# A mixer block's inverse and buffers on one core: second buffers for five tiles, other PSUM banks for late products, and the triangular inverse with its backward half mirrored

## The chip, the core and the metric

One core of a Trainium2 chip runs the whole program. The metric is the device time of one execution in microseconds (us); the time before the change is 2026.64 us, the median of 3 runs (2023.53 to 2029.68).

## What is computed

One layer of a flow-matching backbone over 256 latent tokens and 256 context tokens of width 2048, all in float32. The context tokens are mixed first; each latent scan starts from the context's final state.

```python
o_c, ctx_states = _mix(_modnorm(h_c, norm1_g, m_c[0], m_c[1]), CTX_LEN, zero, lp)
o_x, _ = _mix(_modnorm(h_x, norm1_g, m_x[0], m_x[1]), GRID_W, ctx_states, lp)
h_x = h_x + m_x[2] * o_x
h_x = h_x + m_x[5] * _swiglu(_modnorm(h_x, norm2_g, m_x[3], m_x[4]), ffn_w_gu, ffn_w_down)
return _rmsnorm(h_x, final_g)
```

`_mix` projects the tokens once and splits the result into four groups of 512 channels: GLA (gated linear attention, 4 heads), GDN (gated delta rule, 4 heads), a short gated convolution, and RWKV-7 (8 heads of 64). GLA, GDN and RWKV run forwards and backwards. In the chunked form GDN and RWKV need the solution of a triangular system per chunk:

```python
lmat = where(strict, beta[..., None] * kk * decay, 0.0) + eye(CHUNK)
sol = triangular_solve(lmat, rhs, left_side=True, lower=True, unit_diagonal=True)
```

## The kernel before, in words

**Stages.** Up to some 170 us the kernel streams the modulation weights and the first projections. From there to about 1195 us it mixes (the stage of this change), then multiplies by w_out, normalises, and from some 1290 us runs the feed-forward layer to the end.

**Matmuls in parts.** Weights are split into a high part `wh` (a copy on ScalarE, line 192) and a low part `wl` (a difference on VectorE, line 197) by `split`, lines 248 to 260; a projection (`proj`, lines 589 to 608) is then 48 matmuls of 256 columns into a PSUM tile with tag `big`, and one evacuation.

**Order of the work.** The list `ORDER` (line 41) names the pieces: `rw0` is head pair 0 of RWKV for the context, `RW0` the same for the latents, `gd`, `gl` and `SC` GDN, GLA and the convolution, `pd`, `pr`, `pg` projections that are stored to DRAM for later, `XX0` the change from context to latents (`load_nT`, lines 559 to 585), and `YY0` the point where RWKV's pools close. The framework's scheduler places the instructions of each engine ahead of time: among those whose inputs and buffers are free in its own model it takes the one with the best priority, which is the order of tracing, shifted by the offsets in ORDER. On the chip each queue then runs in that fixed order. A tile with `bufs` 1 has one buffer, and its next use waits until the last reader of the former one is done. `feed` (lines 345 and 599) slips pieces of the later modulation (tag `ob`) between projections.

**PSUM.** Eight banks: `big` 2, `ea` 2, `eb` 1, `la` 1, `lb` 1, `ob` 1 (`PB`, lines 542 to 545). The letter behind e and l is the thread: RWKV uses a, GDN and GLA use b.

**RWKV** (`rwkv`, lines 866 to 1028) handles two heads, in two directions one after the other, 16 directions in all. It prepares the block matrices KK, NB, KB, VB (rings `bd`, one buffer each), multiplies KK by BK into an `ea` bank (line 935), masks the result into `LM` (line 939, ring `bdLM`), copies the turned KK out as `rw_kt` (line 947), turns NB and KB into `rw_na` and `rw_ka`, calls `inverse`, and multiplies the inverse's result `rw_F` by LM (line 972) and by `rw_kt` (line 981). Then a chain of four states follows.

**GDN** (`gdn`, lines 1041 to 1176) handles one head, both directions together, 8 calls in all. `gd_tok` holds the token-major keys and values, `gd_dl` the decays and then the matrix to invert. Behind the inverse it forms `gd_Fb`, `gd_Fg` and the products `pe` (line 1128). **GLA** (`gla`) uses the tags `gd_tok` and `gd_dl` too.

**The inverse** (`inverse`, lines 645 to 740) takes four 128 x 128 units, 24 calls in all (16 of RWKV with the tags `iva`, 8 of GDN with `ivb`). It takes the 16 x 16 diagonal blocks out (lines 655 to 659: one product over 512 columns, one reduction), broadcasts their entries with a matmul into `la` or `lb` (line 670), and solves them in 15 steps of two VectorE instructions on all 128 partitions (lines 677 to 692). In GDN two units are lower and two are upper triangular, so each step is done once per kind, on half the width. Line 694 spreads the 16-column solution to 128 x 512, and two or three levels of matmuls and evacuations build the full inverse. `pxt` (line 732) is the transposed product between GDN's levels.

```python
                    tt(w_[:, u, js], e, Xc[:, u, i:i + 1].to_broadcast([P, len(us), n]), MUL)
                    step.append((u, js))
                for u, js in step:
                    tt(Xc[:, u, js], Xc[:, u, js], w_[:, u, js], ADD)
```

Of the kernel before, what the change touches and what calls it, by code (L numbers as in the profile page):

```python
# [16 lines left out]
P = 128  # L17
# [38 lines left out]
def _const_array():  # L56
# [30 lines left out]
    add("half", np.concatenate([q < 8, q >= 8], 1))  # L87
    r = np.arange(32)[None, :]
# [82 lines left out]
def block_kernel(ctx: ExitStack, tc: tile.TileContext, x, cx, ada_first, ada_later, ada_b, w_in, w_early, w_out,  # L171
# [24 lines left out]
    def tt(o, a, b, op, e=None):  # L196
        (e or V).tensor_tensor(out=o, in0=a, in1=b, op=op)  # L197
# [140 lines left out]
    C = mk(kp, [P, NCONST], "consts")  # L338
    sw = mk(kp, [P, 3072], "sw")

    def cc(name, n=P):
        return C[:, COFF[name]:COFF[name] + n]

# [7 lines left out]
    lo8, hi8 = cc("half", 2)[:, 0:1], cc("half", 2)[:, 1:2]  # L351

# [26 lines left out]
    with ExitStack() as st:  # L379
# [88 lines left out]
        for i, dst in ((0, C), (1, sw)):  # L468
            nc.sync.dma_start(dst, (consts, small)[i])
# [35 lines left out]
    with mix:  # L505
# [139 lines left out]
        def inverse(nL, levels, lowers, rhs=None, out=None, w=P):  # L645
# [6 lines left out]
            for u, low in enumerate(lowers):  # L652
                groups.setdefault(low, []).append(u)

            t5 = mk(mx, [P, 4, 8, 16], iv + "L", 1)
            tt(t5, nL.rearrange("p u (b c) -> p u b c", c=16),
               blk16.unsqueeze(1).unsqueeze(3).to_broadcast([P, 4, 8, 16]), MUL)
            dg = mk(mx, [P, 4, 16], iv + "D", 1)
            V.tensor_reduce(out=dg, in_=t5.rearrange("p u b c -> p u c b"), axis=mybir.AxisListType.X, op=ADD)
# [10 lines left out]
            pr = PB([P, 480], "l")  # L670
# [4 lines left out]
            G.tensor_copy(Xc, bcast(id16, 1, 4))  # L675
            w_ = mk(mx, [P, 4, 16], iv + "w", 1)
            for st in range(15):
                step = []
                for low, us in groups.items():

                    n, u = 15 - st, slice(us[0], us[-1] + 1)
                    if low:
                        i = 15 - st
                        js, e = slice(0, n), bc_[:, u, st, 0:n] if i >= 8 else bc_[:, u, i, 14:14 - n:-1]
                    else:
                        i = st
                        js, e = ((slice(15, i, -1), bc_[:, u, i, 0:n]) if i < 8 else
                                 (slice(i + 1, 16), bc_[:, u, 15 - i, i:15]))
                    tt(w_[:, u, js], e, Xc[:, u, i:i + 1].to_broadcast([P, len(us), n]), MUL)
                    step.append((u, js))  # L690
                for u, js in step:
                    tt(Xc[:, u, js], Xc[:, u, js], w_[:, u, js], ADD)
            X = mk(mx, [P, 4, P], iv + "X", 2)
            tt(X.rearrange("p u (b c) -> p u b c", c=16), bcast(Xc, 2, 8),
               blk16.unsqueeze(1).unsqueeze(3).to_broadcast([P, 4, 8, 16]), MUL)
# [871 lines left out]
```

## Time and profile before

| what | value |
|---|---|
| median of 3 runs | 2026.64 us |
| the profiled execution | 2028.87 us |
| its span in the trace | 2027.1 us |
| TensorE matmul (PE) busy | 1915.4 us, 94% |
| TensorE weight load (PEld) busy | 1633.6 us, 81% |
| VectorE (DVE) busy | 1343.7 us, 66% |
| ScalarE (ACT) busy | 994.5 us, 49% |
| GpSimd (POOL) busy | 161.5 us, 8% |

Matmuls are pipelined and their ends are modelled: a busy PE has a matmul under way, which need not be PE at its peak. In the row of a group, the first number behind the bar is busy time, the second the mean length of one in ns; behind the second bar stands the idle time of the engine just before the group and what ended it. In a timeline row the start and the length stand first. The granted clock is TensorE's, as a share of its full speed.

### The profile page before, as it was taken

The numbers are of one execution on the slowest core, as the hardware profiler recorded it, in microseconds if no ns is written. First come the engines' busy times: TensorE is split into PE (matmuls) and PEld (weight loads), VectorE is DVE, ScalarE is ACT, GpSimd is POOL, SyncE is SP. The second block draws the span as 40 slices with busy tenths as digits, with TensorE's granted clock in tenths as the row PEclk, the third lists the DMA queues.
The fourth block names the chain that finished last, engine by engine and source line by source line (L and its number), as shares of the span: only waits on it lengthen the run. The fifth ranks groups of instructions, "written<-read, shape, count | busy, mean of one in ns | idle before, by whom it ended". The sixth has DMA issues, their size and how long they took to land.

```text
span 2027.1 us, 37228 instructions
## 1 busy us (share of the span) xinstructions
PE 1915.4 (94%) x13799; PEld 1633.6 (81%) x13800; DVE 1343.7 (66%) x3488; ACT 994.5 (49%) x2029; POOL 161.5 (8%) x199
## 2 busy tenths in 40 slices
PE   5988999799999999999999999899999999999998
PEld 3776877588877878989989978788888888888886
DVE  3446758788788758989897766655555555545554
ACT  2225535555455345465644555555555555544444
POOL 0001001001001000110110000210101010100000
PEclk7999999889999999999999999899999999999999
DMA  8976678444566566333233557355555555566654
GB/s 340 402 292 218 181 224 253 118 138 140 168 204 188 156 193 205 115 110 108 82 118 120 168 184 210 116 187 186 187 187 187 187 187 186 186 231 197 191 194 156
DMA packets 162391, 375.07 MB, mean 185 GB/s; under 512 B 17937, under 2 KB 44049, under 8 KB 157089
## 3 DMA queue, kind: packets, MB, share of 16 engines
q1 hardware_dynamic: 156448, 368.42, 55.6%
q10 hardware_dynamic: 5760, 4.27, 0.7%
q8 instruction: 108, 1.77, 0.4%
q14 instruction: 75, 0.61, 0.1%
HBM read 360.68 MB, written 11.94 MB: 184 GB/s over the span
## 4 chain that ended last, share of the span: by engine, by line
PE 69%; DVE 10%; DMA 5%; ACT 3%; issue 2%; POOL 0%; SPq 0%; ACTq 0%; DVEq 0%
PE acc L209 36%; PE big L209 12%; PE la L209 7%; PE lb L209 4%; PE ea L209 4%; DVE wl L197 3%; DMA wraw<-in_w_in 3%; PE eb L209 2%; PE ob L209 2%; ACT wh L192 2%; DMA wraw<-in_ada_later 2%; DVE ivaXc L197 1%; DVE ivaw L197 1%; DVE ivbw L197 0%; DVE ivbXc L197 0%
## 5 line engine op out<-in xcount | busy, mean ns | idle before, releaser
L197 DVE TENSOR_TENSOR wl<-wraw,wh 128x512 fp32r<-128x512 f32 x856 | 569.9, 692 | 425.4 <-ACT wh L192 420.7
L192 ACT ACTIVATE wh<-wraw 128x512 fp32r<-128x512 f32 x856 | 510.1, 625 | 543.6 <-PE acc L209 187.3
L209 PE MATMUL acc<-n,wh 128*128 128x512 f32 x1408 | 493.6, 399 | 2.5 <-ACT wh L192 2.5
L209 PE MATMUL acc<-n,wl 128*128 128x256 f32 x1408 | 383.3, 282 | 0.3 <-DVE wl L197 0.3
L209 PE MATMUL big<-nh,wh 128*128 128x256 f32 x1056 | 320.4, 304 | 1.7 <-ACT xs L192 1.3
L209 PE MATMUL big<-nh,wl 128*128 128x256 f32 x1056 | 309.6, 294 | 1.4 <-DVE wl L197 1.4
L209 PEld LDWEIGHTS acc<-n,wh 128*128 128x128 f32 x1408 | 260.0, 189 | 59.6 <-ACT wh L192 2.8
L209 PE MATMUL big<-nl,wh 128*128 128x256 f32 x1056 | 307.7, 292 | 0.0
L209 PEld LDWEIGHTS acc<-n,wl 128*128 128x128 f32 x1408 | 267.2, 190 | 9.7 <-DVE wl L197 1.3
L209 PEld LDWEIGHTS big<-nh,wh 128*128 128x128 f32 x1056 | 200.4, 190 | 27.2 <-issue 19.4
L209 PEld LDWEIGHTS big<-nh,wl 128*128 128x128 f32 x1056 | 200.3, 190 | 8.0 <-issue 2.9
L209 PEld LDWEIGHTS big<-nl,wh 128*128 128x128 f32 x1056 | 200.2, 190 | 5.2 <-issue 4.1
L209 PE MATMUL acc<-wl,hH 128*128 128x512 f32 x352 | 137.1, 389 | 0.0
L209 PE MATMUL acc<-wh,hH 128*128 128x512 f32 x352 | 137.0, 389 | 0.0
L209 PE MATMUL acc<-wh,hL 128*128 128x512 f32 x352 | 137.0, 389 | 0.0
L209 PE MATMUL ob<-wraw,sc 128*32 128x128 f32 x2048 | 106.4, 281 | 16.0 <-DMA wraw<-in_ada_later 12.4
L209 PEld LDWEIGHTS ob<-wraw,sc 128*32 128x32 f32 x2048 | 51.1, 108 | 52.2 <-DMA wraw<-in_ada_later 18.4
L197 POOL TENSOR_TENSOR hL<-sg,hH 128x256 fp32r<-128x256 f32 x44 | 44.6, 1013 | 454.2 <-ACT hH L192 454.2
L209 PEld LDWEIGHTS acc<-wl,hH 128*128 128x128 f32 x352 | 66.1, 188 | 14.2 <-DVE wl L197 0.4
L209 PEld LDWEIGHTS acc<-wh,hL 128*128 128x128 f32 x352 | 66.1, 188 | 13.8
L209 PEld LDWEIGHTS acc<-wh,hH 128*128 128x128 f32 x352 | 66.1, 188 | 13.7
L197 DVE TENSOR_TENSOR wl<-wr,wh 128x1408 fp32r<-128x1408 f32 x16 | 26.0, 1624 | 42.4 <-ACT wh L192 42.4
(468 smaller groups left out, 3123.9 us busy)
## 6 DMA issues: line engine op xcount, KB each, us to landing
wraw<-in_w_gu SPq DMA_DIRECT2D x174, 512.0 KB, 3.1
wraw<-in_w_in SPq DMA_DIRECT2D x264, 256.0 KB, 3.3
wraw<-in_ada_later SPq DMA_DIRECT2D x256, 256.0 KB, 3.9
wraw<-in_w_down SPq DMA_DIRECT2D x88, 512.0 KB, 3.4
ad<-in_ada_first SPq DMA_DIRECT2D x32, 1024.0 KB, 9.0
wraw<-in_w_out SPq DMA_DIRECT2D x64, 256.0 KB, 2.9
wr<-in_w_early SPq DMA_DIRECT2D x16, 704.0 KB, 9.2
xin<-in_cx SPq DMA_DIRECT2D x2, 1024.0 KB
```

The lines of the kernel that those rows point to most:

```text
L192: A.activation(o, i, AF.Copy)
L197: (e or V).tensor_tensor(out=o, in0=a, in1=b, op=op)
L209: return TE.matmul(o, l, r, start=start, stop=stop)
```

## The change

The three parts of the diff are these.

- Buffers: the ring of LM, `rw_kt`, `rw_na`, `gd_tok` and `gd_dl` get a second buffer. The tile of the constants loses its first 128 columns (the identity has a tile of its own), and the convolution's output uses the tag `y_o` of the other outputs.
- Banks: the inverse's broadcast goes from `la`/`lb` to `ea`/`eb`; the transposed product `pxt` and GDN's `pe` go from `eb` to `big`.
- Inverse: the diagonal blocks are taken out with four copies on ScalarE (32 partitions by 4 x 32 columns each) and two VectorE instructions on 64 columns. The upper units start from an identity with reversed columns, so that all four units go through the same steps, and the spreading (now one instruction per kind) reverses them back.

```diff
@@ -85,6 +85,8 @@
     add("half", np.concatenate([q < 8, q >= 8], 1))
+    add("side", np.concatenate([i // 16 % 2 == 0, i // 16 % 2 == 1], 1))
+    add("id16r", np.arange(P)[:, None] % 16 == 15 - np.arange(16)[None, :])
     r = np.arange(32)[None, :]
@@ -335,11 +337,11 @@
     kp = mix.enter_context(tc.tile_pool(name="kp", bufs=1, reuse_waits="tile"))
-    C = mk(kp, [P, NCONST], "consts")
+    C = mk(kp, [P, NCONST - P], "consts")
     sw = mk(kp, [P, 3072], "sw")
...
     def cc(name, n=P):
-        return C[:, COFF[name]:COFF[name] + n]
+        return C[:, COFF[name] - P:COFF[name] - P + n]
@@ -349,6 +351,8 @@
     lo8, hi8 = cc("half", 2)[:, 0:1], cc("half", 2)[:, 1:2]
+    even, odd = cc("side", 2)[:, 0:1], cc("side", 2)[:, 1:2]
+    id16r = cc("id16r", 16)
@@ -466,7 +470,7 @@
         for i, dst in ((0, C), (1, sw)):
-            nc.sync.dma_start(dst, (consts, small)[i])
+            nc.sync.dma_start(dst, (consts[:, P:], small)[i])
         for f in done:
@@ -652,11 +656,13 @@
-            t5 = mk(mx, [P, 4, 8, 16], iv + "L", 1)
-            tt(t5, nL.rearrange("p u (b c) -> p u b c", c=16),
-               blk16.unsqueeze(1).unsqueeze(3).to_broadcast([P, 4, 8, 16]), MUL)
+            dq = mk(mx, [P, 4, 32], iv + "Q", 1)
+            for q in range(4):
+                sl = slice(32 * q, 32 * q + 32)
+                acopy(dq[sl], nL[sl, :, sl])
             dg = mk(mx, [P, 4, 16], iv + "D", 1)
-            V.tensor_reduce(out=dg, in_=t5.rearrange("p u b c -> p u c b"), axis=mybir.AxisListType.X, op=ADD)
+            ts(dg, dq[:, :, 0:16], even, MUL)
+            stt(dg, dq[:, :, 16:32], odd, dg, MUL, ADD)
@@ -667,32 +673,27 @@
-            pr = PB([P, 480], "l")
+            pr = PB([P, 480])
             mm(pr, ones16, sel.rearrange("p u i j -> p (u i j)"))
...
             Xc = mk(mx, [P, 4, 16], iv + "Xc", 1)
-            G.tensor_copy(Xc, bcast(id16, 1, 4))
+
+            for low, us in groups.items():
+                G.tensor_copy(Xc[:, us[0]:us[-1] + 1], bcast(id16 if low else id16r, 1, len(us)))
             w_ = mk(mx, [P, 4, 16], iv + "w", 1)
             for st in range(15):
-                step = []
-                for low, us in groups.items():
-
-                    n, u = 15 - st, slice(us[0], us[-1] + 1)
-                    if low:
-                        i = 15 - st
-                        js, e = slice(0, n), bc_[:, u, st, 0:n] if i >= 8 else bc_[:, u, i, 14:14 - n:-1]
-                    else:
-                        i = st
-                        js, e = ((slice(15, i, -1), bc_[:, u, i, 0:n]) if i < 8 else
-                                 (slice(i + 1, 16), bc_[:, u, 15 - i, i:15]))
-                    tt(w_[:, u, js], e, Xc[:, u, i:i + 1].to_broadcast([P, len(us), n]), MUL)
-                    step.append((u, js))
-                for u, js in step:
-                    tt(Xc[:, u, js], Xc[:, u, js], w_[:, u, js], ADD)
+
+                n = i = 15 - st
+                e = bc_[:, :, st, 0:n] if i >= 8 else bc_[:, :, i, 14:14 - n:-1]
+                tt(w_[:, :, 0:n], e, Xc[:, :, i:i + 1].to_broadcast([P, 4, n]), MUL)
+                tt(Xc[:, :, 0:n], Xc[:, :, 0:n], w_[:, :, 0:n], ADD)
             X = mk(mx, [P, 4, P], iv + "X", 2)
-            tt(X.rearrange("p u (b c) -> p u b c", c=16), bcast(Xc, 2, 8),
-               blk16.unsqueeze(1).unsqueeze(3).to_broadcast([P, 4, 8, 16]), MUL)
+            for low, us in groups.items():
+                us_ = slice(us[0], us[-1] + 1)
+                tt(X[:, us_].rearrange("p u (b c) -> p u b c", c=16),
+                   bcast(Xc[:, us_] if low else Xc[:, us_, ::-1], 2, 8),
+                   blk16.unsqueeze(1).unsqueeze(3).to_broadcast([P, len(us), 8, 16]), MUL)
             nxt = iv + "XT", 1 if len(levels) == 2 and rhs is not None else 2
@@ -729,7 +730,7 @@
                 if not last and (rhs is None or b != levels[-2]):
-                    pxt = PB([P, 4, P])
+                    pxt = PB([P, 4, P], "big")
                     for c in range(4):
@@ -797,7 +798,7 @@
                 V.tensor_copy(er[32:40, d, 0:2], smd[d][32:40, (127 if d == 0 else 0):T:P])
-            esel = C[32:40, COFF["esel"]:COFF["esel"] + 32].rearrange("p (r c) -> p r c", c=4)
+            esel = C[32:40, COFF["esel"] - P:COFF["esel"] - P + 32].rearrange("p (r c) -> p r c", c=4)
             et = mk(mx, [P, 8, 4], "get", 1)
@@ -943,12 +944,12 @@
                     TE.transpose(pk[:, c], f2(KK[:, c]), ident)
-                kt_ = mk(mx, [P, 4, P], "rw_kt", 1)
+                kt_ = mk(mx, [P, 4, P], "rw_kt", 2)
                 acopy(kt_, pk)
...
                 def turned(t, tag):
-                    pt, o = PB([P, 4, P]), mk(mx, [P, 4, P], tag, 1)
+                    pt, o = PB([P, 4, P]), mk(mx, [P, 4, P], tag, 2 if tag == "rw_na" else 1)
                     for c in range(4):
@@ -1064,7 +1065,7 @@
                 l2(q, P ** -0.5)
-            tok = mk(mx, [P, 4, P], "gd_tok", 1)
+            tok = mk(mx, [P, 4, P], "gd_tok", 2)
             pt = PB([P, 4, P])
@@ -1084,7 +1085,7 @@
                 mm(pbc[:, d], ident[:, 32 + r:33 + r].to_broadcast([P, P]), sm["smd"][d])
-            dl = mk(mx, [P, 4, P], "gd_dl", 1)
+            dl = mk(mx, [P, 4, P], "gd_dl", 2)
             R = mk(mx, [P, 4, 2, P], "gd_R", 1)
@@ -1125,7 +1126,7 @@
                     ts(Fg[:, u].rearrange("p a b -> p (a b)")[:, :w], src, sm["nbe"][:, d, h, c:c + 1], MUL)
-                pe = PB([P, 2, 2, P])
+                pe = PB([P, 2, 2, P], "big")
                 for c in range(2):
@@ -1179,7 +1180,7 @@
             if s == 1:
-                v = mk(mx, [P, 4, 2, 64], "gd_tok", 1)
+                v = mk(mx, [P, 4, 2, 64], "gd_tok", 2)
                 for hh in range(2):
@@ -1195,7 +1196,7 @@
             else:
-                v = mk(mx, [P, 2, 2, P], "gd_tok", 1)
+                v = mk(mx, [P, 2, 2, P], "gd_tok", 2)
                 for hh in range(2):
@@ -1222,7 +1223,7 @@
                         TE.transpose(pt[:, c], ke[:, c * P:(c + 1) * P], ident)
-                    kt_ = mk(mx, [P, 4, P], "gd_dl", 1)
+                    kt_ = mk(mx, [P, 4, P], "gd_dl", 2)
                     acopy(kt_[:, :2], pt)
@@ -1255,7 +1256,7 @@
                     TE.transpose(pt[:, c], KE[:, c].rearrange("p a b -> p (a b)"), ident)
-                kt_ = mk(mx, [P, 4, P], "gd_dl", 1)
+                kt_ = mk(mx, [P, 4, P], "gd_dl", 2)
                 acopy(kt_, pt)
@@ -1277,7 +1278,7 @@
             f4 = lambda t: t.rearrange("p c h j -> p (c h j)")
-            sq = mk(mx, [P, 512], "gd_tok", 1)
+            sq = mk(mx, [P, 512], "gd_tok", 2)
             act(sq, f4(y), AF.Square)
@@ -1297,7 +1298,7 @@
             conv(o, pr, [pc("scconv", tap * 4 + t) for tap in range(3)], 1)
-            yo = t1("sc_y", 2)
+            yo = t1("y_o", 2)
             tt(yo, pcol(nHL, "c_b", t), o, MUL)
@@ -1338,7 +1339,7 @@
         rings = rws.enter_context(tc.tile_pool(name="rings", bufs=1, reuse_waits="tile"))
-        bdLM = Ring(rings, "bdLM", [P, 4, 2, 2, 64], 1)
+        bdLM = Ring(rings, "bdLM", [P, 4, 2, 2, 64], 2)
         bdKh = Ring(rings, "bdKh", [P, 4, 2, 64], 1)
```

## Rows read from the trace of the kernel before

**Rows 1.** The page's chain that ended last: shares of the span by engine

```profile
PE 69%; DVE 10%; DMA 5%; ACT 3%; issue 2%; POOL 0%; SPq 0%; ACTq 0%; DVEq 0%
```

**Rows 2.** The same chain in order of time: start us, us, what

```profile
409.27 2.09 PE la L209 x8
...
1287.32 730.15 PE acc L209 x3822
```

**Rows 3.** Busy time per stretch: us, PE, PEld, DVE, ACT, POOL, clock, DMA share, GB/s

```profile
170.00:1200.00 1030.00, 973.94 (x8342) 842.62 (x8339) 811.32 (x2561) 534.37 (x1145) 88.68 (x116) 0.98 0.52 161
...
335.00:450.00 115.00, 98.01 (x759) 80.14 (x760) 90.98 (x281) 63.83 (x152) 6.28 (x11) 0.87 0.48 147
450.00:800.00 350.00, 335.52 (x3179) 281.39 (x3171) 270.39 (x905) 172.75 (x369) 27.39 (x40) 1.00 0.59 183
800.00:1100.00 300.00, 288.59 (x2194) 267.81 (x2194) 260.95 (x836) 158.13 (x330) 33.87 (x42) 1.00 0.33 103
```

**Rows 4.** Timeline around two hand-overs between RWKV directions: start us, us, engine, operation

```profile
557.79 1.16 PE L209 MATMUL ea<-rw_BK,bd 128*128 128x128 f32 x8
...
578.59 1.10 PE L209 MATMUL la<-rw_F,bdLM 128*128 128x64 f32 x8
...
580.62 1.39 DVE L197 TENSOR_TENSOR bdLM<-ea,consts 64x512 f32<-64x512 f32 x2
...
581.03 1.00 PE L209 MATMUL la<-rw_F,rw_kt 128*128 128x64 f32 x8
...
582.07 0.60 ACT L192 ACTIVATE rw_kt<-ea 128x512 f32<-128x512 f32 x1 [1.70 <-PE la L209]
...
1033.05 1.16 PE L209 MATMUL la<-rw_F,bdLM 128*128 128x128 f32 x8
...
1037.09 0.67 DVE L197 TENSOR_TENSOR bdLM<-ea,consts 64x512 f32<-64x512 f32 x1
```

**Rows 5.** Groups of VectorE instructions, 200 to 1200 us

```profile
L197 DVE TENSOR_TENSOR ivaXc<-ivaXc,ivaw 128x60 f32<-128x60 f32 (+14 forms) x240 | 48.1, 200 | 2.3
...
L197 DVE TENSOR_TENSOR ivbw<-ivbC,ivbXc 128x30 f32<-128x30 f32 (+14 forms) x240 | 33.6, 168 | 0.8 <-ACT ivbC L192 0.7
...
L197 DVE TENSOR_TENSOR ivaL<-bdLM,consts 128x512 f32<-128x512 f32 x48 | 33.8, 704 | 0.0
...
L659 DVE TENSOR_REDUCE ivaD<-ivaL 128x64 f32<-128x512 f32 x16 | 16.4, 1025 | 0.1
...
L206 DVE SCALAR_TENSOR_TENSOR ivad<-ivaD,consts,ivad 128x60 f32<-128x60 f32 x16 | 4.4, 274 | 0.0
...
L201 DVE TENSOR_SCALAR ivad<-ivaD,consts 128x60 f32<-128x60 f32 x16 | 3.9, 246 | 0.1
...
L197 DVE TENSOR_TENSOR ivaXT<-la,rw_na 128x256 f32<-128x256 f32 x8 | 3.4, 424 | 7.0 <-PE la L209 6.7
...
L206 DVE SCALAR_TENSOR_TENSOR gd_R<-ident,gdec,eb 128x128 f32<-128x128 f32 x32 | 10.3, 342 | 5.6 <-PE lb L209 2.9 <-PE eb L209 2.6
```

**Rows 6.** Groups of ScalarE instructions by form, 200 to 1200 us

```profile
L192 ACT ACTIVATE bd<-rw_v 64x256 f32<-64x256 f32 x28 | 11.5, 412 | 2.1 <-DVE rw_v L206 1.6 <-DVE ivbw L197 0.3
L192 ACT ACTIVATE gd_S<-lb 128x128 f32<-128x128 f32 x24 | 6.6, 274 | 15.9 <-PE lb L209 15.8
...
L192 ACT ACTIVATE xs<-big 128x256 f32<-128x256 f32 x55 | 20.3, 374 | 9.9 <-PE big L209 6.8 <-issue 3.0
L192 ACT ACTIVATE ivbXT<-eb 128x512 f32<-128x512 f32 x16 | 9.5, 595 | 4.7 <-PE eb L209 3.9 <-PE ea L209 0.7
```

**Rows 7.** PE's waits, 200 to 1200 us: us in total, times, longest us

```profile
PE la L700 <- DVE ivaX L197: 2.8, 4, 1.4
PE lb L700 <- DVE ivbX L197: 2.2, 3, 0.9
...
PE lb L209 <- DVE ivbR L197: 2.1, 1, 2.1
```

**Rows 8.** PE's waits for an emptied projection bank, 450 to 1100 us

```profile
PE big L209 <- ACT xs L192: 1.1, 2, 0.9
```

## The prediction

> **What bounds the kernel now.** I read the page's chain first. It runs 69% on PE, 10% on VectorE (DVE), 5% on transfers and 3% on ScalarE (ACT) [rows 1]. In order of time its last piece is one unbroken run of 730 us of feed-forward matmuls from 1287 us on [rows 2]; nothing of the change touches those, so all that can move lies ahead, in the mixing stage. The busy time per stretch says how full that stage is: in the 1030 us from 170 to 1200 us PE is busy 973.9, DVE 811.3, ACT 534.4 us, so PE's idle time is 56.1 us in all [rows 3]. It is uneven: 17.0 us of it lie in the 115 us around the change from context to latents (335 to 450 us), where the granted clock is 0.87 as well; 14.5 us in the next 350 and 11.4 us in the next 300.
>
> The timeline shows what holds an RWKV direction back. The product KK x BK of the next direction ends in its `ea` bank at 558.9 us, but the masked copy into LM starts at 580.6 us, after the former direction's last product with the old LM (578.6 to 579.7 us); likewise `rw_kt` is written at 582.1 us, right after the last matmul that reads the old one [rows 4]. For 21 us two full PSUM banks wait for one buffer each, and the next inverse can't start. The last hand-over, at 1033 to 1037 us, has the same order [rows 4]. No engine's row shows this as a wait, since the queues are laid out around it. So the stage is one long serial thread (RWKV), a second one (GDN, GLA), and projections that fill PE between them.
>
> **The change part by part.** The sum is made against the profiled execution (2028.87 us; span 2027.1 us and 1.8 us around it), which lies 2.2 us above the median of the runs, 2026.64.
>
> *VectorE's work in the inverse.* Taking out the diagonal costs a product of 0.704 and a reduction of 1.025 us, 24 times: 41.5 us. In their place come two instructions on 64 columns; the nearest rows are those on 60 columns, 0.246 and 0.274 us [rows 5], 12.5 us in all. GDN's steps are two lists of 240 instructions at 0.168 us, 80.6 us; one pass over all four units is 240 instructions of RWKV's width, at 0.200 us [rows 5], 48.0 us. The spreading in GDN becomes two instructions of 256 columns (0.424 us) for one of 0.704: plus 0.14 us, 8 times, 1.2 us. Sum for DVE: -29.0 - 32.6 + 1.2 = -60.4 us. ACT gets 96 copies of 32 x 128. No row has this form; a 128 x 128 copy out of PSUM takes 0.274 us and one of 64 x 256 in SBUF 0.412 [rows 6]. I take the middle, 0.34 us, as the copy has the columns of the one and the source of the other: 32.9 us, with ends of 26 and 40.
>
> How much of that reaches the end? The chain has 203 us on DVE (10% of 2027), a quarter of its 811 us, and 61 us on ACT, 11% of 534 [rows 1, 3]. In those shares the gain is 60.4 x 0.25 - 32.9 x 0.11 = 11.5 us. From the other side: PE's own idle time put down to the end of these very pieces (`ivaX`, `ivbX`, `ivbR`) is 7.1 us [rows 7]. PE has other work during the rest, so I take -6 us, with ends of -11.5 and +3.6 (ACT's share alone, no gain).
>
> *Second buffers.* The LM copy can go some 21 us earlier, at 559 us, and with it `rw_kt`, `rw_na`, the diagonal and the steps of the next inverse, while the former one is in its levels. But PE was busy in those 21 us with projections, and its instructions stay the same. What can be won is its idle time: 25.9 us from 450 to 1100 us [rows 3]. I take a third, -8 us, since part of those waits belongs to transfers and evacuations that stay; ends 0 and -25.9. Next in line is `rw_ka`, which keeps one buffer: its product waits in one of the two `ea` banks until the former direction has used the old one. `gd_tok` and `gd_dl` get the same freedom on the GDN thread; it starts a head far less often, so I cost them at nothing, covered by RWKV's thread, and with that gone they are in the same ends.
>
> *The change-over at 335 to 450 us.* Here no projection can fill PE (the latents' input is being made), but context heads of RWKV, GDN and GLA are ready and held by single buffers. PE idles 17.0 us, and a mean clock of 0.87 means 0.26 of the 115 us, 30 us, at the lower of the two levels, which costs busy matmuls up to 15 us [rows 3]: eight matmuls take 2.09 us at 409 us [rows 2] and 1.16 us at 1033 us [rows 4]. More overlap would fill PE and perhaps keep the clock up. Much of the idle time waits for x itself, so I take -4 us; ends -15 (the clock holds), +8 (work runs out earlier and the low stretch grows by half).
>
> *Banks.* The broadcast moves to `ea`/`eb`, which frees `la` for the chain of states; `ea` has two banks, one of them more often full. 32 GDN tiles (two `pxt` and two `pe` in each of 8 calls) go to the two projection banks. Each is held for some eight matmuls (1.16 us) and an evacuation of 0.595 us on ACT [rows 6] or four instructions of 0.342 on DVE [rows 5], 1.8 to 2.5 us, in which projections have one bank and pay their own evacuation (0.374 us [rows 6]) in the open unless other work stands next in PE's queue. Today PE waits 1.1 us in all for such an evacuation from 450 to 1100 us [rows 8]. Ends: -4 (what `eb` gives back) and +20 (32 x 0.6, evacuation and hand-over each time); I take +2, near today's row.
>
> *The rest.* No transfer is added, and none moves in SP's queue or another; the one that loads the constants gets 110 columns (56 KB) shorter, behind the early weights: nothing. GDN's POOL copy becomes two of half size; POOL is busy 88.7 of 1030 us [rows 3], and they run under the extraction, which covers them: nothing, or without that cover 8 of POOL's mean instruction (88.7/116 = 0.76 us [rows 3]), 6 us. The convolution's output now shares two buffers with the others: four tiles, each freed by a copy and a difference of some 0.4 us (the lengths for 256 columns in [rows 5, 6]), so 0 to +3 us; I take 0, as w_out's projections follow.
>
> Sum: -6 - 8 - 4 + 2 = -16 us, so 2012.9 us as a profiled execution, 2010.6 us against the median.
>
> **The rivals.**
>
> *Nothing (2026 us, between 2021 and 2033).* PE is 95% busy in the stage, and its matmuls stay. What is late may only change its name: `rw_ka`, KK's ring and the `ea` banks still have to turn over. For it: in the rows of before, PE waited 7.1 us on the parts that get shorter. Against it: 56 us of idle time and a low clock, which a fuller queue can use. That the second LM buffer is given but not used earlier, because the scheduler's order keeps the copy behind, belongs here. By the Trainium skill, TensorE: Matmul & The Clock Gate, section HAM oscillation, a kernel whose K loop already kept PE warm gained nothing from double-buffered PSUM. That is this rival; here the trace agrees from 450 us on (clock 1.00) and not before.
>
> *Much more (1991 us).* "Busy" counts each matmul to its modelled end, and single matmuls behind a wait leave room inside it. PEld is busy 842.6 of 1030 us, so 187 us are free by that measure [rows 3]. With the thread's period cut by part of the 21 us, the ends of the first three parts come in: -11.5 - 13 - 11 = -35.5 us, so 1991 us. Against it: from 800 to 1100 us DVE is busy 261 of 300 us and would bind next [rows 3]. The Trainium skill, Perfetto Trace Analysis, section Identifying the Most-Contended Engine, holds that weight loads, not matmul busy time, tell TensorE's headroom; by it the bound would be 187 us and not 56.
>
> *Slower (2036 us): the projection banks.* With GDN's 32 tiles in them and the scheduler's model placing projections right behind, each hold stops PE for 0.8 us: 32 x 0.8 = 25.6 us on top of the forecast. It decides from 0.5 us a hold on (16 us, all of the gain). For it: two banks are all that projections have, 1.8 to 2.5 us a hold, and the offsets in ORDER were set for other lengths. Against it: PE has other threads' matmuls to run, and only 1.1 us go to this wait today.
>
> **How the numbers follow.** Forecast 0.48, much more 0.15, nothing 0.19, slower 0.18. What a measurement of this kernel can tell from no change is about 0.3%, 6 us: faster means under 2020.6, slower over 2032.7. The forecast and the large gain are faster, 0.63; nothing is 0.19; the banks 0.18. The range of 1990 to 2036 takes in the large gain and the centre of the slow case, and leaves out some 0.07 below and 0.1 above.
>
> **What would show it.** Right: the LM copy stands well ahead of the former direction's last LM product; the reductions are gone and GDN's step lists count 120 each; PE's idle time from 170 to 1200 us falls from 56 to some 40 us; the last feed-forward run begins near 1271 us. Wrong: `big` rows with waits for ACT or DVE evacuations of GDN tiles; a longer low clock between 380 and 440 us; idle time that stays at 56 us under new names, `rw_ka` above all.

## The result, and the profile after

The changed kernel takes 2205.49 us (median of 4 runs, 2203.72 to 2208.27) against 2027.06 us of the kernel before beside it: a ratio of 1.0883 [1.0862, 1.0903], 178 us slower. The profiled execution of after is 2204.72 us, with a span of 2202.9 us. Lines stand a little further down than before (L209 is now L211, L197 is L199, L192 is L194, SP's store of a projection is L625, not L621).

Page of after, busy time and chain:

```profile
PE 1990.6 (90%) x13799; PEld 1665.5 (76%) x13800; DVE 1331.3 (60%) x3256; ACT 1032.2 (47%) x2125; POOL 155.3 (7%) x208
...
PE 72%; DVE 12%; DMA 7%; ACT 5%; issue 2%; POOL 1%; SPq 0%; ACTq 0%; DVEq 0%; POOLq 0%
```

The number of matmuls is the same, and VectorE is hardly less busy (1331.3 us for 1343.7). The same chain in order of time (start, us, what) shows where the loss ends:

```profile
1462.55 707.53 PE acc L211 x3726
```

Before, that run began at 1287.32 us [rows 2]: 175.2 us later, of 175.9 us between the two profiled executions. The feed-forward layer is as it was; all of the loss lies ahead of it. Busy time per stretch of after (columns as in [rows 3]):

```profile
170.00:1200.00 1030.00, 883.83 (x7172) 722.38 (x7171) 697.76 (x2139) 484.75 (x1072) 76.87 (x120) 0.91 0.42 132
335.00:450.00 115.00, 97.48 (x742) 75.29 (x742) 88.37 (x277) 70.22 (x167) 8.43 (x13) 0.87 0.44 136
450.00:800.00 350.00, 301.17 (x2573) 246.08 (x2573) 217.90 (x684) 148.37 (x319) 19.86 (x37) 0.91 0.42 133
800.00:1100.00 300.00, 250.80 (x1891) 211.41 (x1891) 212.22 (x615) 145.36 (x317) 28.25 (x41) 0.92 0.36 112
1100.00:1150.00 50.00, 36.43 (x194) 30.48 (x194) 38.03 (x138) 12.49 (x28) 2.85 (x4) 0.76 0.00 0
```

In the 1030 us PE does 1170 matmuls fewer than before (7172 for 8342 [rows 3]); its idle time is 146.2 us instead of 56.1, and the granted clock falls from 0.98 to 0.91. No one engine took over: DVE, ACT and the DMA share fell as well. From 1100 to 1150 us hardly anything is moved (0 GB/s in the row), although weights remain to be fetched. Something keeps the projections back.

PE's timeline in after, the rows that write a projection bank (`big`) around two stretches without projections:

```profile
630.23 0.28 PE L211 MATMUL big<-nh,wl 128*128 128x256 f32 x1
...
731.64 0.70 PE L211 MATMUL big<-gd_Fg,gd_tok 128*128 128x256 f32 x2
731.99 0.47 PE L211 MATMUL big<-nh,wh 128*128 128x256 f32 x1
...
1018.05 0.28 PE L211 MATMUL big<-nh,wl 128*128 128x256 f32 x1
...
1164.57 0.65 PE L211 MATMUL big<-gd_Fg,gd_tok 128*128 128x256 f32 x2
1164.87 0.47 PE L211 MATMUL big<-nh,wh 128*128 128x256 f32 x1
```

For 102 and for 147 us no projection runs (`nh` and `nl` are its inputs), and each time the first one follows a `pe` product of a GDN call by 0.3 us. Three more stretches end behind `pe` in the same way: 303 to 358, 458 to 538 and 931 to 972 us. The view of the tile `big` says what it holds in the longest of them, 1018.3 to 1170 us (the projections' few rows left out):

```profile
L211 PE MATMUL big<-ivbW,ivbX x32: 275/275/421, 1054.6 to 1150.7; 128*128 128x128 f32 x32
...
L211 PE MATMUL big<-gd_Fg,gd_tok x16: 379/380/483, 1067.6 to 1166.5; 128*128 128x256 f32 x16
```

These are four `pxt` and four `pe` tiles of two GDN calls. From its first product to the end of its last read each holds a bank for 1.7 to 5.8 us, some 26 us in all, one bank at a time: both banks stand empty most of the 147 us. So they are not held; they are reserved. The trace of before has the rows that say so in advance. SP's queue stores the last twelve projections (`PG`) from 907 to 1060 us, and PE's `pe` of GD3, which ORDER lists ahead of `PG1 PG0`, comes behind them:

```profile
906.58 0.45 SPq L621 DMA_DIRECT2D xr_g_k<-xs  x1
...
1060.07 0.42 SPq L621 DMA_DIRECT2D xr_g_r<-xs  x1
...
1084.66 0.59 PE L209 MATMUL eb<-gd_Fg,gd_tok 128*128 128x256 f32 x2
```

Before, a projection traced behind a GDN call could overtake it, since it used other banks. In after the same twelve are stored from 1179.63 to 1261.43 us, behind that `pe`:

```profile
1179.63 0.39 SPq L625 DMA_DIRECT2D xr_g_k<-xs  x1
...
1261.43 0.33 SPq L625 DMA_DIRECT2D xr_g_r<-xs  x1
```

The other latent GDN calls show the same. In after, the projections (by their stores) and the calls' `pe` products come in the order of the list: PD0 PR0, GD0, PR1 PD3 PD1 PR2 PR3, GD1, PD2, GD2, GD3, PG1 PG0. Before, PD2's first store (850.00 us) stands ahead of GD1's first `pe` (875.60 us); in after it stands behind it, at 982.51 against 965.20 us.

### The profile page after: what moved, and what is told of

Same layout as the page of the kernel before. It is cut to its first block, busy times and chain, and to the rows that moved or that the text cites. A ratio compares the mean times of both kernels' runs of the same rounds, so it can differ in the third digit from the quotient of the medians.

```text
span 2202.9 us, 37120 instructions
## 1 busy us (share of the span) xinstructions
PE 1990.6 (90%) x13799; PEld 1665.5 (76%) x13800; DVE 1331.3 (60%) x3256; ACT 1032.2 (47%) x2125; POOL 155.3 (7%) x208
## 4 chain that ended last, share of the span: by engine, by line
PE 72%; DVE 12%; DMA 7%; ACT 5%; issue 2%; POOL 1%; SPq 0%; ACTq 0%; DVEq 0%; POOLq 0%
PE acc L211 36%; PE big L211 14%; PE la L211 7%; PE ea L211 4%; DMA wraw<-in_w_in 4%; PE lb L211 3%; DVE wl L199 3%; PE ob L211 2%; ACT wh L194 2%; PE eb L211 2%; DMA wraw<-in_ada_later 2%; DVE ivaXc L199 1%; DVE ivaw L199 1%; DMA yr<-Yd 1%; PE pt L211 0%
## 5 line engine op out<-in xcount | busy, mean ns | idle before, releaser
L199 DVE TENSOR_TENSOR wl<-wraw,wh 128x512 fp32r<-128x512 f32 x856 | 568.7, 691 | 517.0 <-ACT wh L194 514.4
L194 ACT ACTIVATE wh<-wraw 128x512 fp32r<-128x512 f32 x856 | 510.1, 626 | 579.2 <-PE acc L211 188.1
L211 PE MATMUL acc<-n,wh 128*128 128x512 f32 x1408 | 493.1, 399 | 3.0 <-ACT wh L194 3.0
L211 PE MATMUL acc<-n,wl 128*128 128x256 f32 x1408 | 382.6, 282 | 0.3 <-DVE wl L199 0.3
L211 PE MATMUL big<-nh,wh 128*128 128x256 f32 x1056 | 315.4, 299 | 9.7 <-DVE y_o L199 4.4
L211 PE MATMUL big<-nh,wl 128*128 128x256 f32 x1056 | 309.3, 293 | 2.0 <-DVE wl L199 2.0
L211 PE MATMUL big<-nl,wh 128*128 128x256 f32 x1056 | 305.9, 290 | 0.0
L211 PEld LDWEIGHTS acc<-n,wh 128*128 128x128 f32 x1408 | 259.7, 189 | 60.0 <-ACT wh L194 3.4
L211 PEld LDWEIGHTS acc<-n,wl 128*128 128x128 f32 x1408 | 266.8, 189 | 9.2 <-DVE wl L199 0.8
L211 PEld LDWEIGHTS big<-nh,wh 128*128 128x128 f32 x1056 | 202.4, 192 | 29.6 <-issue 13.3
L211 PEld LDWEIGHTS big<-nh,wl 128*128 128x128 f32 x1056 | 202.2, 192 | 8.5 <-DVE wl L199 4.5
L211 PEld LDWEIGHTS big<-nl,wh 128*128 128x128 f32 x1056 | 202.5, 192 | 5.2 <-issue 4.8
L211 PE MATMUL ob<-wraw,sc 128*32 128x128 f32 x2048 | 115.4, 294 | 32.3 <-DMA wraw<-in_ada_later 28.0
L211 PE MATMUL acc<-wl,hH 128*128 128x512 f32 x352 | 137.2, 390 | 0.6 <-DVE wl L199 0.6
L211 PE MATMUL acc<-wh,hH 128*128 128x512 f32 x352 | 137.1, 390 | 0.0
L211 PE MATMUL acc<-wh,hL 128*128 128x512 f32 x352 | 137.0, 389 | 0.0
L211 PEld LDWEIGHTS ob<-wraw,sc 128*32 128x32 f32 x2048 | 49.7, 111 | 78.5 <-DMA wraw<-in_ada_later 41.8
L211 PEld LDWEIGHTS acc<-wl,hH 128*128 128x128 f32 x352 | 66.1, 188 | 15.2 <-DVE wl L199 1.3
L211 PEld LDWEIGHTS acc<-wh,hH 128*128 128x128 f32 x352 | 66.1, 188 | 14.2 <-ACT wh L194 0.3
L199 POOL TENSOR_TENSOR hL<-sg,hH 128x256 fp32r<-128x256 f32 x44 | 44.5, 1012 | 453.7 <-ACT hH L194 453.7
L211 PEld LDWEIGHTS acc<-wh,hL 128*128 128x128 f32 x352 | 66.1, 188 | 13.5
L199 DVE TENSOR_TENSOR ivaw<-ivaC,ivaXc 128x60 f32<-128x60 f32 (+14 forms) x240 | 47.2, 197 | 10.5 <-ACT ivaC L194 7.4
```

Of the source, the lines that this page charges most:

```text
L194: A.activation(o, i, AF.Copy)
L211: return TE.matmul(o, l, r, start=start, stop=stop)
```

## Theories

A: the buffers of a tag go round in the order of tracing, so with `pxt` and `pe` in `big` every projection traced behind a GDN call has to take its turn behind that call's late products, however early its weights and inputs are there. B: each late tile holds a bank for its own length (my rival "slower"). C: the second buffers or the new inverse are the cause.

## Experiments

All ratios are against the kernel before, run beside each. Differences of over 20 us are between the medians, smaller ones the ratio's share of 2026 us.

**e1: the late products back in `eb`**, in the changed kernel.

```diff
-                    pxt = PB([P, 4, P], "big")
+                    pxt = PB([P, 4, P])
...
-                pe = PB([P, 2, 2, P], "big")
+                pe = PB([P, 2, 2, P])
```

> The changed kernel with GDN's pxt and pe back in eb; second buffers, the broadcast's bank and the new inverse stay. Theory A: the buffers of a tag are given out in the order of tracing, so a projection traced behind a GDN call gets its big bank only after that call's last product has had one; all of the loss is this. Then the time falls from 2205 to near or below the kernel before: 1995 to 2030 us, and no gap over 20 us is left in the projections between 600 and 1150 us. Theory C: the second buffers let RWKV's thread run ahead and leave the projections for later, so the loss stays: over 2120 us. Theory B (the banks are held too long) expects here the same as A.

2069.48 us, 1.0202 [1.0179, 1.0224]: 136 us of the 178 are gone, and with them all five stretches. But 43 us stay over the kernel before, more than A's 1995 to 2030 us allowed.

**e2: only these two edits, in the kernel before.**

> The kernel before with nothing changed but GDN's pxt and pe in big. Theory A: at least the loss of the whole change, 2160 to 2240 us, with gaps in the projections that end at a matmul of pxt. Theory C: no part of the loss, 2015 to 2045 us. Theory B: 32 tiles at 0.8 us each, 2040 to 2065 us.

2221.61 us, 1.0954 [1.0912, 1.0997], with stretches of 57, 99, 98, 42 and 160 us, each ended by a `pe` (I had expected a `pxt`). The end of the longest, PE's rows on `big`:

```profile
1199.65 0.70 PE L209 MATMUL big<-gd_Fg,gd_tok 128*128 128x256 f32 x2
1200.00 0.47 PE L209 MATMUL big<-nh,wh 128*128 128x256 f32 x1
```

That is A, and neither B (2040 to 2065 us) nor C.

**e3: a bank of their own**, in the changed kernel: projections get one bank, `pxt` and `pe` the other (and of w_out's two accumulators there, one goes to each).

```diff
-            tag = tag if tag == "big" else tag + cur[0]
-            return mk(pb, shape, tag, 2 if tag in ("big", "ea") else 1)
+            tag = tag if tag in ("big", "bg") else tag + cur[0]
+            return mk(pb, shape, tag, 2 if tag == "ea" else 1)
...
-                    pxt = PB([P, 4, P], "big")
+                    pxt = PB([P, 4, P], "bg")
...
-                pe = PB([P, 2, 2, P], "big")
+                pe = PB([P, 2, 2, P], "bg")
```

> The changed kernel with the two big banks parted: projections have one, GDN's pxt and pe the other (w_out's first accumulators use one of each). Theory A: the lists of waiting tiles are parted too, so most of the loss is gone although projections have half the banks: 2020 to 2090 us (80 projections, each with its evacuation of 0.4 to 0.7 us in the open). Theory B: fewer banks cost more, so 2205 us or above.

2084.14 us, 1.0276 [1.0248, 1.0305]. With half the banks the projections lose 121 us less than with two shared ones. So it is the order in the tag that costs, not the number of banks or the time they are held.

**e4: one call later in the order**, in the changed kernel: `GD3 PG1 PG0` becomes `PG1 PG0 GD3`.

> The changed kernel with one word of ORDER moved: GD3 is traced behind PG1 and PG0 instead of ahead of them. The banks, their number and how long they are held stay. Theory A: the twelve projections of PG need no longer wait for GD3's last product and fill the empty stretch from 1020 to 1180 us; they are 12 x 48 matmuls of some 0.12 us, 69 us, so 2120 to 2160 us. Theory B and theory C: no change, 2190 to 2215 us.

2184.15 us, 1.0770 [1.0737, 1.0802]. The stretch of 147 us shrinks to 54 (1020.5 to 1074.8 us) and now ends with GD2's `pe`, as A says. Of its 93 us only 21 reach the end: GD3 is now late itself (its last `pe` is at 1214 us for 1166 in after), and GLA's last output comes at 1304 us for 1323. The size was missed.

**e18: only `pxt` in `big`**, in the kernel before.

> The kernel before with pxt alone in big (pe stays in eb). Theory A: projections wait until a call's last pxt instead of its last pe. With both in big the five gaps of the projections that end at a pe product end at 353, 553, 754, 991 and 1200 us, and the last pxt products of those calls stand at 342, 541, 737, 977 and 1185 us, 12, 12, 17, 16 and 17 us earlier in the first matmul's time: 74 us less loss than the 195 us there, so about 2147, 2115 to 2180. Rival B (each late tile holds a bank): half of the tiles, half of the loss: 2125 by its own measure only if it could explain 195 us for both, 2030 to 2045 by hold times.

2210.30 us, 1.0914 [1.0882, 1.0947]. PE's rows on `big` in this run:

```profile
1170.49 0.61 PE L209 MATMUL big<-ivbW,ivbX 128*128 128x128 f32 x4
1170.86 0.36 PE L209 MATMUL big<-nh,wh 128*128 128x256 f32 x1
```

Each stretch now ends with a `pxt`, so the wait is set by the last shared product. But the number was wrong: against e2 the stretches are 65 us shorter in sum (46, 85, 81, 23 and 156 us) and the time only 11, between medians of two runs each. A stretch's length is not its price. The profiled executions of e2 and e18 are 16 us apart, and w_out's first weights are issued 16 us earlier (1346.5 for 1362.8 us), so the gain fits what is still undone when the last stretch ends; no run tests that by itself.

**e6: the convolution's output in `y_o`, and nothing else**, in the kernel before.

```diff
-            yo = t1("sc_y", 2)
+            yo = t1("y_o", 2)
```

> The kernel before with one edit: the convolution's output takes the tag y_o. Theory A: its tiles that are traced behind GLA's last call get a y_o buffer only once GLA's outputs there are written; the last of them comes some 40 to 50 us later, w_out with it, time 2050 to 2080. Rival B, and my forecast of 0 to +3 us for this part: 2024 to 2032.

2069.53 us, 1.0194 [1.0173, 1.0216]: 42 us, nearly the 43 that e1 left. DVE's timeline, the rows that write the tile:

```profile
1194.58 0.42 DVE L197 TENSOR_TENSOR y_o<-gd_qe,gd_q 128x256 f32<-128x256 f32 x1
1194.92 0.41 DVE L197 TENSOR_TENSOR y_o<-big,xs 128x256 f32<-128x256 f32 x1
```

`gd_qe` is GLA's last output and `big,xs` the convolution's. With a tag of its own the latter was written at 1138 us, while GLA still worked:

```profile
1138.11 0.42 DVE L197 TENSOR_TENSOR sc_y<-big,xs 128x256 f32<-128x256 f32 x1
...
1199.65 0.42 DVE L197 TENSOR_TENSOR y_o<-gd_qe,gd_q 128x256 f32<-128x256 f32 x1
```

`SC2 SC3 SC1` are traced behind `GL1`, so their buffers come behind its own. Meanwhile both projection banks stay full: the next instructions that read one start at 1194.92 and 1195.37 us, no projection starts between 1142.80 and 1195.39 us, and PE runs dry. The stretch from 1150 to 1200 us in e6, then before:

```profile
1150.00:1200.00 50.00, 27.87 (x104) 21.71 (x105) 20.46 (x52) 14.85 (x36) 2.24 (x2) 0.52 0.03 9
```

```profile
1150.00:1200.00 50.00, 48.80 (x291) 40.49 (x290) 36.73 (x79) 31.44 (x66) 4.47 (x4) 1.00 0.58 186
```

**e5: both put right**, in the changed kernel: e1, `sc_y` again, and `gd_tok` with one buffer for the room.

> The changed kernel with pxt and pe back in eb, the convolution's output back under a tag of its own (sc_y, two buffers), and gd_tok with one buffer, which frees the room for that. Theory A (whatever is traced behind a tile of a shared tag waits for that tile, however early it is ready): of the 43 us that stayed over the kernel before when only pxt and pe went back, nearly all is the shared y_o: the convolution's three tiles for the end of the list no longer wait for GLA's last outputs, w_out starts near 1150 us again and not at 1207, time 2000 to 2030. Rival B (what stays is the price of the new inverse or of the second buffers): still over 2050.

2040.25 us, 1.0066 [1.0053, 1.0079], missing A's range by 10 us. The two shared tags make up 165 of the 178 us, 136 for the banks (e1) and 29 for `y_o` (with `gd_tok`'s second buffer, which this run drops too). The remaining 13 us are a loss where I had forecast a gain, so the parts were run alone.

**e7: the new inverse alone**, in the kernel before, on the old banks.

> The kernel before with the new inverse alone (diagonal by ScalarE copies, all four units in the same steps, two spreadings); the banks stay as before (broadcast in la or lb, pxt in eb), all buffers too. My forecast for this part: -6 us with ends -11.5 and +3.6, so 2015 to 2030, most likely 2020; VectorE's busy time some 60 us lower, ScalarE's some 33 us higher. Rival B (the 43 us that stayed come from the inverse): 2050 to 2075.

2040.12 us, 1.0072 [1.0046, 1.0098]: slower by 15 us, although DVE's busy time falls by 28.4 us (1343.7 to 1315.3). The trace is of an execution of 2054.99 us, 15 us above the median, so its waits say less than the times.

**e8: four of the second buffers alone.**

> The kernel before with second buffers for LM, rw_kt, rw_na and gd_dl alone (gd_tok keeps one, as the room is short); the constants' tile shortened as in the change. My forecast for this part: -8 us with ends 0 and -25.9, so 2001 to 2027, most likely 2018 (with the change-over's -4: 2014). Rival B (the 43 us come from here): 2050 to 2075.

2046.13 us, 1.0089 [1.0076, 1.0103]: slower by 18 us. SP's waits say where, from 440 to 1100 us, first before, then e8 (L621 stores a projection):

```profile
SPq L621 <- ACT xs L192: 22.4, 17, 5.5
```

```profile
SPq L597 <- DVE wl L197: 104.8, 42, 13.9
SPq L621 <- ACT xs L192: 71.7, 23, 26.9
```

and SP's timeline in e8:

```profile
638.96 0.43 SPq L627 DMA_DIRECT2D rw_rraw<-xr_r_r  x1
648.66 0.32 SPq L621 DMA_DIRECT2D xr_d_k<-xs  x1
660.25 0.32 SPq L533 DMA_DIRECT2D rw_S<-sd_rw  x1
663.01 0.24 SPq L305 DMA_DIRECT2D gated<-wraw  x1
663.52 0.33 SPq L597 DMA_DIRECT2D wraw<-in_w_in  x1
```

RWKV's thread is ahead there (its ninth inverse result at 648 us, not 670), but a store waits for its projection until 648.7 us, a state load until 660.3 us, and no weights of a projection are issued behind them until 663.5 us.

**e10: e8 with the two waiting kinds of transfer on other queues; e11: the same two moves in the kernel before.**

```diff
-            nc.sync.dma_start(t, SD[key])
+            G.dma_start(t, SD[key])
...
-            nc.sync.dma_start(dst, t)
+            A.dma_start(dst, t)
```

> The kernel with the four second buffers, and in addition the store of a projection (spill) issued from ScalarE's queue, behind the copy that fills it, and the load of a state (get_state) from GpSimd's, so that neither can stand in SP's queue ahead of weights. Theory D (the buffers let the RWKV thread run ahead, and its stores and state loads, placed earlier in SP's queue than they can run, hold back the weight loads behind them: 72 us of SP's waits are for a copy into xs, against 22 before, and no weight load is issued from 638 to 663 us): SP's waits for xs go, the dip of PE from 650 to 700 us goes, time 2015 to 2032. Rival E (the loss is PE's order itself, with projections placed too late): no change, 2040 to 2052.

> The kernel before with the same two moves of DMA issues and nothing else. Theory D: SP's queue waits 22 us for copies into xs here, in pieces up to 5.5 us, and the weights have room for most of it: 2015 to 2030. If it falls by as much as the kernel with second buffers does, the moves are a gain by themselves and say nothing on the buffers.

e10: 2028.31 us, 1.0008 [0.9994, 1.0022]; e11: 2028.88 us, 1.0012 [1.0002, 1.0022]. The moves give the kernel before nothing and take 16 us from the one with second buffers. No wait of SP for `xs` is left in e10, and the pause in the projections from 648 to 668 us in e8 is gone. The stretch from 650 to 700 us in e8, then in e10:

```profile
650.00:700.00 50.00, 43.76 (x356) 36.16 (x357) 35.68 (x150) 16.66 (x33) 1.76 (x4) 0.90 0.34 108
```

```profile
650.00:700.00 50.00, 48.43 (x501) 41.03 (x500) 40.00 (x159) 18.54 (x37) 3.14 (x5) 1.00 0.64 210
```

So theory D holds for the buffers: their loss goes with the waits in SP's queue. Which of the two moves does it was not tested. Without the loss the buffers are worth nothing that can be measured: e10 and e11, which differ in the buffers alone, are 0.6 us apart. The Trainium skill (Trainium Kernel Development and Optimization, Key Constraints) says that issuing DMAs from several engines saves the sequencer's issue time only. For the kernel before that agrees with e11; in e10 it saved what stood waiting ahead of the weights, and the measurement decides.

**e9: the broadcast's bank alone** (`pr` in `ea`/`eb`, in the kernel before).

> The kernel before with one edit: the inverse's broadcast goes to ea/eb instead of la/lb. My forecast for this (with the late products) was +2 us, -4 at best. Theory A (order behind a shared tag): eb is also where GDN's and GLA's other products turn over, in the thread's own order, so little is changed in who waits for whom: 2018 to 2036. Rival: over 2040, then this too is a part of what the inverse with all of its banks costs.

2026.18 us, 0.9997 [0.9989, 1.0006]: nothing.

**e12, e13: the moves of the queues on e5 and on e7.**

> The changed kernel with pxt and pe in eb, the convolution's output under its own tag and gd_tok with one buffer, and the two moves of DMA issues. Theory D: the 13 us that it stood above the kernel before go, and the gain that I forecast for the inverse and the buffers (-6 and -12) shows: 2005 to 2030. Rival E: 2035 to 2045.

> The kernel before with the new inverse alone, and the two moves of DMA issues (spills on ScalarE's queue, state loads on GpSimd's). Theory D (SP's queue: in the trace of the new inverse alone SP waits 41.6 us for copies into xs, and PE's clock falls to 0.66 from 280 to 300 us): 2020 to 2032. Rival F (the loss is the order of the work that the scheduler makes of the new lengths, on all queues): 2033 to 2045.

e12: 2039.39 us, 1.0060 [1.0046, 1.0074]. e13: 2037.32 us, 1.0048 [1.0032, 1.0064]. Both missed. In e7 SP does wait longer for stores (one of 17.5 us, where the longest was 5.5), but most of the inverse's loss stays when stores and state loads have left SP's queue. That falls in F's range and not in D's.

**e14, e15: the inverse's halves alone; e16: the same work in another order** (`GD0:-100 RW0:50` becomes `GD0:-80 RW0:30`).

> The kernel before with the new steps alone (reversed identity, one list for all four units, two spreadings); the diagonal is taken out as before. Work: VectorE 32 us less, PE and ScalarE the same. Theory F: anything from 2018 to 2042, set by the order; my forecast's share for this would be some -3 us, 2023. Rival G (the ScalarE copies are what costs): no loss here, 2018 to 2030.

> The kernel before with the new way to take the diagonal out alone (four ScalarE copies and two VectorE instructions per call), the steps as before. Work: VectorE 29 us less, ScalarE 29 us more. Rival G: the whole loss, 2036 to 2045. Theory F: anything from 2018 to 2042; if this and the steps alone are both even, the loss is no property of either.

> The kernel before with two numbers in the list of the order changed by 20 (GD0 from -100 to -80, RW0 from 50 to 30), so with the same instructions in another order. Theory F: it moves by several us in either direction although nothing is done differently, 2015 to 2050, and not within 3 us of the kernel before. Rival: within 3 us, 2023 to 2029.

e14: 2022.27 us, 0.9981 [0.9970, 0.9993]; e15: 2025.57 us, 0.9996 [0.9984, 1.0008]; e16: 2026.01 us, 1.0001 [0.9989, 1.0013]. Neither half costs anything, so G falls. The steps alone come out 3.8 us lower, clear of 1 by their interval; but e11, which changes no work, lies 2.4 us above, clear of 1 as well, so a difference of this size is not shown to be the work of the steps. And a small change of priorities costs nothing, so F as I put it, that any new order moves the time by several us, falls too.

**e17: the steps, the buffers and the moves together.**

> The kernel before with the new steps of the inverse, the four second buffers (LM, rw_kt, rw_na, gd_dl), and the two moves of DMA issues; the diagonal, all banks and the convolution's tag as before. If the parts add up: -3.5 us (steps alone) and +1 to +2.5 us (buffers with the moves), so 2021 to 2026. If the buffers let the shorter steps count (my forecast's reasoning: less VectorE work shows where a thread can start early): 2005 to 2018. If the combination makes a worse order, as the inverse's two halves did: over 2030.

2033.23 us, 1.0045 [1.0030, 1.0061]. Parts of -3.8 and +1.6 us make +9. As with the inverse's halves, the loss belongs to the combination (the steps with the moves, without the buffers, were not run). What makes it was not found: it stays open.

## Why the prediction was wrong

The step that failed is "Banks", and the rival "Slower" with it. Both priced how long a late tile holds a bank, 0.6 or 0.8 us for each of 32; the place was right and the mechanism wrong. What costs is the order in which a tag's buffers are given out: projections that had run up to 178 us ahead of GD3's products had to come behind them. That took 136 us out of the changed kernel when put right (e1) and put 195 us into the kernel before (e2), where my ends were -4 and +20. The sentence "Against it: PE has other threads' matmuls to run" failed too: in those stretches the threads leave PE gaps, and its clock falls (PE busy 36.43 of 50 us at 0.76 from 1100 to 1150 us).

"The rest" failed in the same way: I priced the shared `y_o` by its readers, 0 to +3 us, and took 0 "as w_out's projections follow". It costs 42 us in the kernel before (e6) and 29 in the changed one (e1 to e5), since the convolution's tiles stand behind GLA's in the tag.

"Second buffers": the mechanism was seen rightly. In after, the LM copy of the third context pair is at 389.27 us, ahead of the former direction's last LM product:

```profile
389.27 0.69 DVE L199 TENSOR_TENSOR bdLM<-ea,consts 64x512 f32<-64x512 f32 x1
...
403.55 1.10 PE L211 MATMUL la<-rw_F,bdLM 128*128 128x64 f32 x8
```

But -8 us became +18 alone (e8) and +1.6 with SP's queue out of the way (e10): PE's idle time there was not won, as the 0 end allowed, and the work moved earlier put its transfers in SP's queue ahead of weights. What the prediction cites from the Trainium skill (TensorE: Matmul & The Clock Gate, HAM oscillation), that PSUM double-buffering gave no further gain where PE is kept warm, is about PSUM, and the second buffers here are in SBUF. They gave none either in e10, at a clock of 1.00 from 450 to 1100 us; for PSUM no run here tests it alone. (The prediction has this trace agree from 450 us on "and not before"; from 170 to 335 us the clock was 0.99 as well, and only the change-over was low.) I had written that no transfer moves in SP's queue; none is moved by the diff, but a thread that gets ahead takes its stores and loads along. "Change-over", -4: the clock from 335 to 450 us is 0.87 in after as before; with e5's edits it is 0.94 and PE's idle time 18 us for 17, so the idle time did not shrink. What the better clock gave was not measured apart, and e5 as a whole is no faster.

"VectorE's work": -60.4 us for DVE was far too much. The page gives -28.4 for the whole inverse (e7), -19.0 for the diagonal (e15, forecast -29.0), -6.9 for the steps with the spreading (e14, forecast -31.4). For the steps the reason stands in [rows 5]: 240 of 168 ns are 40.3 us, the row's busy time is 33.6, since narrow neighbours overlap, and I multiplied. The products and updates of GDN's steps together keep DVE busy for 58.9 us before and 45.5 in e14, so they save 13.4 us and not 32.6. The diagonal was sized rightly: its own rows in e15 are 28 us shorter, and why the page's total falls by 19.0 only is open. (The page's figure is itself good to some 5 us: e8 and e9, with the same VectorE work as before, have 1348.6 and 1346.7.) The steps of after, 200 to 1300 us:

```profile
L199 DVE TENSOR_TENSOR ivbw<-ivbC,ivbXc 128x60 f32<-128x60 f32 (+14 forms) x120 | 23.1, 192 | 7.2 <-ACT ivbC L194 5.4
...
L194 ACT ACTIVATE ivaQ<-bdLM 32x128 f32<-32x128 f32 x62 | 18.9, 305 | 5.3 <-DVE bdLM L199 4.6
```

So the row for the products of GDN's steps shrinks by 10.5 us, 33.6 to 23.1, where count times mean gave 16.3 (half of 32.6). ScalarE's copies take 0.305 us, within my ends of 26 and 40 us for 96 (0.27 to 0.42 us each). Of the forecast of -6 us the steps alone give 3.8 at most (e14), the diagonal none, and both together cost 15.

"Nothing" gave the reason that the matmuls stay and what is late changes its name; that is what the buffers alone showed (e10). "Much more" was out of reach, and its sum does not follow from the text: 13 and 11 us are not the ends given for the second and third part, 25.9 and 15. The sign I set for "Slower", waits on `big` for evacuations, would not have found it: PE isn't waiting for an evacuation but runs in an order made beforehand, in which the projection stands behind `pe`. The holds of the sum, 1.8 to 2.5 us, were too short as well: up to 5.8 us in the longest stretch, and 28 us for GD0's second `pe` tile (731.64 to 760.00 us), during which projections went on in the other bank. That e3, with half the banks, is 121 us faster shows that holding is not where the time went.

## What to carry to other kernels

Before a tile gets another's tag, read in the trace which of the two kinds of tile runs ahead of its place in the program, and by how much: from then on neither overtakes the other, and that lead, not the time for which a buffer is held, tells how large the price can get (here a lead of up to 178 us cost 136 to 195 us, one of some 60 us 29 to 42). A thread that is allowed to run ahead takes its transfers along in a queue that keeps its order; where the trace shows them waiting ahead of weights, they belong on a queue that carries none (16 us from e8 to e10, nothing in e11). Parts that cost nothing alone can cost together, so measure them together, and take an engine's saving from busy time in a row, not from count times mean.

## What the runs showed of the hardware

Nothing that contradicts the rows of before. The granted clock answered to PE's gaps as it did at the change-over: 0.76 from 1100 to 1150 us in after and 0.52 from 1150 to 1200 us in e6, where PE was busy 28 of 50 us and the transfers had all but stopped (9 GB/s).
